# Both layers' overflow parts in front of their last groups, another passage between the layers and a shorter reciprocal root

## The chip, the cores and the metric

The kernel runs on one core of a Trainium2 chip. The metric is the device time of one execution in microseconds (us), the median of several. A profile is one further execution, recorded instruction by instruction. PE (TensorE) does matrix products and PEld its weight loads, DVE is VectorE, ACT is ScalarE, POOL is GpSimd, and SP is SyncE, which here only issues DMAs and reads addresses. [...]

## The reference

A backbone of two layers, 256 context tokens and 256 latent tokens of 1024 features, all in float32. Each layer is a token mixer and then a mixture of experts (MoE), both behind a modulated RMS norm and added to the stream through a gate row (`g2` is the MoE's, one row for the context tokens and one for the latent ones):

```python
def rmsnorm(t, g):
    y = t * rsqrt(mean(t * t, axis=-1) + 1e-6)
    return y * g

def hier_moe(h, ...):                 # 32 experts; each token gets 2 experts of its best group of 8
    for e in range(32):
        hid = silu(t @ w_gate[e]) * (t @ w_up[e])         # 1024 -> 256
        y = y + gates[:, e:e + 1] * (hid @ w_down[e])     # 256 -> 1024
    ...
# layer 0: context and latent tokens (512); layer 1: the MoE sees the latent tokens only (256)
x = x + g2 * hier_moe(modnorm(x, norm_g, sh2, sc2), ...)
# after both layers: rmsnorm(x, final_g)
```

## The kernel before

The stream `X` stays on the chip in tiles of 128 tokens: tiles 0 and 1 are the context, 2 and 3 the latent tokens. Layer 0's MoE works on four tiles (T = 4), layer 1's on two. An `Identity` matrix turns a 128x128 block on TensorE (`tr`, line 246); `mm` is an ordinary product (line 242).

**The MoE stage** is the loop over groups at the end of `tail` (from line 1528). A group is one product of 128 rows: two experts with 64 rows each (letters `s`, `p` of `SEQ`) or four with 32 rows each (`q`). Layer 0 has 13 groups, layer 1 has 11. Tokens are put into the rows by rank within their expert. `pair` (line 1731) does one group: the first products with the gate and up weights (PSUM tile `psg`), SiLU on ScalarE and a product on VectorE, `then` (the next group's rows, `rows(q + 1)`), the transposes of the hidden rows and their copy `hidT`, the down product (`psm`), the rows scaled by their gates and split into a high and a low part, and the products that bring the rows back to their tokens (`psc`), added to an accumulator `F` in each group but the last.

In the last group the local `gated()` (line 1542) multiplies the accumulated `F` by `g2` and adds it to `X`, a background step that `pair` issues behind the group's SiLU, and `add` (line 1549) takes the last group's own part: layer 1 has `g2` in the rows already (`cols`), layer 0 multiplies each returned 128x512 block by `g2` (line 1553) and adds it to `X` (line 1554), three of them on GpSimd (`SHARE`).

**The weights** come in units of 1 MB (three per expert: gate and up in two, down in one). `weights`, `pump` and `expert_load` (lines 1586 to 1592 and around) issue them on SyncE's DMA queue in the order of use, one as soon as a unit is given back by a product that is done with it. The first experts (`FIXED`) have a fixed place; the others are ordered by how many tokens they got, so SyncE reads each one's number from the chip's memory (`values_load`) before its first load.

**The overflow part** (`overflow`, line 1615) serves tokens whose rank lies above the rows of a group. It reads the largest count (line 1618), and under `tc.If(cnt > 64)` (line 1621) it goes through all 32 experts again, with the last five or six weight units as its memory, which it loads again at its end. In this run the count is below that and the body is skipped: each engine reads the count and jumps. What stands ahead of the `If` in the program is done ahead of it on each engine; the scheduler (Tile) that orders the instructions mixes nothing across it, and the semaphore counts that its body would move are brought up to date on the other path. Layer 0's is called at line 1497, ahead of group 0, where `F` is still empty (hence the branch `if not F`, which adds to `X` directly); layer 1's at line 1529, ahead of group 2 (`OVER`).

**Other work that the change touches.** `norm1` (line 439) makes the turned, normalised rows of all four tiles at the start of each layer: sum of squares, `rsqrt_`, scaling on VectorE (line 453), turning on TensorE, evacuation with the modulation. `rsqrt_` (line 169) is a reciprocal root on VectorE, an integer first guess and two steps of iteration, ten instructions on columns of one to ten numbers; `rms` feeds it, and `final` (line 1809) uses it for the output. `s5_prepare` is work for layer 1's mixer, laid into layer 0's last groups as background (`self.bg`); `prefetch1` starts layer 1's loads behind layer 0's last group.

Of the kernel before, what the change touches and what calls it, by code (L numbers as in the profile page):

```python
# [13 lines left out]
I32 = mybir.dt.int32  # L14
U32 = mybir.dt.uint32
AF = mybir.ActivationFunctionType
ALU = mybir.AluOpType
# [4 lines left out]
P = 128  # L22
# [6 lines left out]
OVER = (0, 2)  # L29
EARLY = (4, 4)  # L30
SHARE = ((0, 0), (1, 0), (2, 0))
# [130 lines left out]

def small(pool, name, n):

    return pool.tile([P, 10], F32, name=name, tag=name)[:, :n]


def rsqrt_(nc, pool, src, n, scale, src2=None):


    V = nc.vector
    x, y, t, q = (small(pool, "rs" + c, n) for c in "xytq")
    if src2 is None:
        V.tensor_scalar(x, src, float(scale), EPS, op0=ALU.mult, op1=ALU.add)
    else:
        V.scalar_tensor_tensor(x, src, EPS, src2, op0=ALU.add, op1=ALU.add)
    V.tensor_scalar(y.bitcast(I32), x.bitcast(I32), -0.5, float(0x5F375C00), op0=ALU.mult, op1=ALU.add)
    V.scalar_tensor_tensor(t, y, -0.5, y, op0=ALU.mult, op1=ALU.mult)
    V.tensor_mul(t, t, x)
    V.scalar_tensor_tensor(y, t, 1.5009, y, op0=ALU.add, op1=ALU.mult)  # L180
    V.tensor_mul(t, y, y)
    V.tensor_mul(t, t, x)
    V.tensor_scalar(q, t, 0.375, -1.25, op0=ALU.mult, op1=ALU.add)
    V.tensor_mul(q, q, t)
    V.scalar_tensor_tensor(y, q, 1.875, y, op0=ALU.add, op1=ALU.mult)
    return y
# [44 lines left out]
class Body:  # L231
# [193 lines left out]
    def rms(self, tiles, tmp):  # L425

        n = len(tiles)
        if n == 1:
            ss = small(self.sm, "ss", 2)
            for h in range(2):  # L430
                cs = slice(512 * h, 512 * h + 512)
                self.nc.scalar.activation(tmp[0], self.X[tiles[0]][:, cs], AF.Square, scale=1.0 / 32, accum_out=ss[:, h:h + 1])
            return rsqrt_(self.nc, self.sm, ss[:, 0:1], 1, 1.0, ss[:, 1:2])
        ss = small(self.sm, "ss", n)
        for j, i in enumerate(tiles):
            self.nc.scalar.activation(tmp[j], self.X[i][:], AF.Square, accum_out=ss[:, j:j + 1])
        return rsqrt_(self.nc, self.sm, ss, n, 1.0 / D)

    def norm1(self, layer):
# [9 lines left out]
        for b in range(2):  # L449
            xn = [next(ring) for _ in range(2)]  # L450
            r = self.rms([2 * b, 2 * b + 1], xn)
            for i in range(2):
                nc.vector.tensor_scalar(xn[i], self.X[2 * b + i][:], r[:, i:i + 1], None, op0=ALU.mult)  # L453
            for j in range(4):
# [3 lines left out]
                for k in range(4):  # L458
                    d, i = 2 * j + k // 2, k % 2
                    self.tr(ps[:, 128 * k:128 * k + 128], xn[i][:, 128 * d:128 * d + 128])  # L460
# [895 lines left out]
    def tail(self, layer, tiles, mix, mixT):  # L1356
# [5 lines left out]
        with ExitStack() as es:  # L1362
# [133 lines left out]
            if not local:  # L1496
                self.overflow(layer, h2d, T, None)
                ask(1)
# [28 lines left out]
            for q in range(nG):  # L1527
                if local and q == OVER[layer]:
                    self.overflow(layer, h2d, T, F)
# [7 lines left out]
                gate2 = lambda t: row(g2, 0 if local else t // 2)  # L1537
                if q == nG - 1:

                    def gated():  # L1540
                        for n, t in enumerate(tiles):
                            V.tensor_mul(F[n], F[n], gate2(t))
                            V.tensor_add(self.X[t][:], self.X[t][:], F[n])
                            yield
                    self.work(1000)
                    self.bg = gated()

                    def add(n, cs, ps):
                        t = tiles[n]
                        if local:  # L1550
                            V.tensor_add(self.X[t][:, cs], self.X[t][:, cs], ps)
                            return
                        V.tensor_mul(F[n][:, cs], gate2(t)[:, cs], ps)
                        (nc.gpsimd if (n, cs.start) in SHARE else V).tensor_add(self.X[t][:, cs], self.X[t][:, cs], F[n][:, cs])
# [5 lines left out]
                               (row(g2, 0), row(g2, 1)) if local and final else None, q == 0 and not local)  # L1560
# [54 lines left out]
    def overflow(self, layer, h2d, T, F):  # L1615
# [3 lines left out]
        last = 5 if F else 6  # L1619
        assert len(self.pre) - last >= self.first[OVER[layer]]  # L1620
        with tc.If(cnt > 64):  # L1621
# [4 lines left out]
            if layer == 0:  # L1626
                self.route_places(T)
            nc.gpsimd.memset(x, 0.0)
            if not F:
                g2 = self.pre[-6].f  # L1630
                for b in range(2):
                    self.mod_row(layer, b, 5, g2[:, D * b:D * b + D])

                def F(n, cs, ps):
                    V.tensor_mul(ps, g2[:, D * (n // 2):D * (n // 2) + D][:, cs], ps)
                    V.tensor_add(self.X[n][:, cs], self.X[n][:, cs], ps)
# [94 lines left out]
    def pair(self, q, xT, T, part, n, tokc, gate, F, work=0, after=0, then=None, cols=None, new=False):  # L1731
# [24 lines left out]
        self.cp(hidT, ps[:, :256].rearrange("p (k t) -> p k t", t=128))  # L1756
# [49 lines left out]
    def final(self):  # L1806
# [4 lines left out]
        for t in (2, 3):  # L1811
            u = self.unit()
            y.append(u.f[:, :D])
            for h in range(2):
                nc.scalar.activation(u.f[:, D:D + 512], self.X[t][:, 512 * h:512 * h + 512], AF.Square, scale=1.0 / 32, accum_out=ss[:, k:k + 1])
                k += 1
# [226 lines left out]
```

## Time and profile before

| | |
|---|---|
| median of 3 runs | 1200.01 us (1198.22 to 1200.25) |
| the profiled execution's own time | 1194.71 us |
| its span, first to last instruction | 1192.7 us |
| TensorE, VectorE, ScalarE, GpSimd busy | 91 %, 59 %, 27 %, 4 % of the span |
| granted TensorE clock, mean | 0.963 |
| DMA | 298.82 MB, mean 251 GB/s |
| layer 0's MoE groups | about 385 to 690 us |
| layer 1's MoE groups | about 943 to 1187 us |

The shares are means over stages with different limits; the page also cuts the span into 40 equal slices (29.8 us each), where a digit is the busy share in tenths. The chain of waits goes back from the last instruction, at each step to what released it. A timeline lists instructions of one engine in order of time: start, length, what it is (output <- inputs by the program's names, shapes), the count where several alike stand in a row, and the idle time ahead with what ended it. The view of one line gives for each queue and instruction the count, the ns (min/median/max), and the first and last start. A table of stretches gives start:end, length, the busy us of PE, PEld, DVE, ACT and POOL (with counts), the granted clock, the DMA share and GB/s. Groups give count | busy us, mean ns | idle us before, with the releaser.

### The profile page before, as it was taken

The page shows a single profiled execution, that of the slowest core. Times are in us where ns is not written, and L with a number is a line of the kernel's source. Part 1 is how long each engine was busy: PE and PEld are TensorE (multiplying, and loading weights), DVE is VectorE, ACT ScalarE, POOL GpSimd, SP SyncE. Part 2 cuts the span into 40 slices and gives each one's busy share as a digit, 9 for nine tenths or more (in the row PEclk, how much of TensorE's full clock was granted, in tenths as well). Part 3 has the DMA queues.
Part 4 walks back from the last instruction along what each step waited for, and adds up shares of the span by engine and source line. Part 5 has one row for each costly group of instructions (what it writes and reads, how often), then busy time and mean ns, then how long its engine had stood idle before and what let it go on. Part 6 is the DMA issues. An engine that isn't in the chain of part 4 may idle for free.

```text
span 1192.7 us, 17395 instructions
## 1 busy us (share of the span) xinstructions
PE 1087.7 (91%) x6528; PEld 560.3 (47%) x6528; DVE 699.0 (59%) x1915; ACT 319.2 (27%) x651; POOL 52.6 (4%) x64
## 2 busy tenths in 40 slices
PE   5999999999998899989989879999989899999975
PEld 2356556544456333334435246556665554444331
DVE  4876889558567375363453678857564554433324
ACT  3323212135123211120221065245442221212111
POOL 0001410000000100000000100010000000000000
PEclk9999999959999899999999889999989899999998
DMA  8777533640404589999798512345637285999994
GB/s 306 283 266 265 212 131 129 239 196 4 173 36 135 206 349 419 421 419 413 294 421 320 208 36 75 121 137 201 231 137 292 83 342 229 422 421 421 420 420 190
DMA packets 48601, 298.82 MB, mean 251 GB/s; under 512 B 6407, under 2 KB 8984, under 8 KB 15165
## 3 DMA queue, kind: packets, MB, share of 16 engines
q1 hardware_dynamic: 40380, 281.58, 60.4%
q10 hardware_dynamic: 5728, 11.86, 2.7%
q0 software_dynamic: 2400, 4.19, 1.0%
q8 instruction: 54, 0.88, 0.3%
q14 instruction: 39, 0.31, 0.1%
HBM read 295.68 MB, written 4.26 MB: 251 GB/s over the span
## 4 chain that ended last, share of the span: by engine, by line
PE 45%; DVE 10%; DMA 9%; ACT 2%; issue 1%; DVEq 0%; SPq 0%; ACTq 0%
PE psg L242 15%; PE psm L242 13%; PE psc L242 11%; DMA big<-w_e 9%; PE pst L242 3%; PE pst L246 2%; DVE big L1280 1%; PE psc L825 1%; DVE big L1216 1%; DVE big L1147 1%; DVE fr L1773 1%; ACT fr L1772 0%; DVE big L254 0%; ACT big L1155 0%; DVE big L1212 0%
## 5 line engine op out<-in xcount | busy, mean ns | idle before, releaser
L242 PE MATMUL psm<-big 128*128 128x512 f32 (+8 forms) x672 | 197.7, 466 | 4.6 <-ACT big L256 2.4
L242 PE MATMUL psg<-big,big 128*32 128x512 f32 (+1 forms) x720 | 176.6, 618 | 9.6 <-DMA big<-w_e 9.6
L242 PE MATMUL psm<-big,big 128*32 128x64 f32 (+7 forms) x600 | 129.2, 446 | 8.0 <-DVE big L254 4.1
L242 PEld LDWEIGHTS psm<-big 128*128 128x128 f32 (+2 forms) x672 | 91.3, 166 | 87.8 <-issue 64.7
L242 PE MATMUL psc<-big 128*32 128x32 f32 (+8 forms) x1108 | 111.6, 268 | 17.3 <-ACT big L514 7.8
L242 PE MATMUL psg<-big 128*64 128x512 f32 (+1 forms) x264 | 95.6, 617 | 8.1 <-PEq L1621 6.7
L242 PEld LDWEIGHTS psc<-big 128*32 128x32 f32 (+3 forms) x1108 | 73.7, 128 | 56.2 <-issue 29.7
L242 PE MATMUL psc<-fr 128*128 128x512 f32 x296 | 94.0, 431 | 4.1 <-DVE fr L1773 3.1
L1786 DVE TENSOR_TENSOR big<-big,psc 128x512 f32<-128x512 f32 x128 | 82.6, 684 | 22.0 <-PE psc L242 21.5
L246 PE MATMUL pst<-k_par,big 128*128 128x128 f32 (+2 forms) x470 | 80.5, 299 | 15.8 <-DVE big L453 3.7
L246 PEld LDWEIGHTS pst<-k_par,big 128*128 128x128 f32 (+2 forms) x470 | 55.8, 149 | 68.0 <-issue 30.1
L242 PEld LDWEIGHTS psc<-fr 128*128 128x128 f32 x296 | 49.5, 187 | 76.8 <-DVE big L1786 20.3
L242 PEld LDWEIGHTS psg<-big,big 128*32 128x32 f32 (+1 forms) x720 | 44.2, 124 | 86.2 <-issue 69.8
L242 PEld LDWEIGHTS psm<-big,big 128*32 128x32 f32 (+2 forms) x600 | 54.0, 145 | 51.8 <-issue 39.2
L1773 DVE SCALAR_TENSOR_TENSOR fr<-psm,tab,fr 128x512 fp32r<-128x512 f32 x46 | 34.6, 751 | 74.1 <-ACT fr L1772 71.7
L256 ACT ACTIVATE big<-pst 128x512 f32<-128x512 f32 (+2 forms) x88 | 47.3, 547 | 92.2 <-PE pst L246 85.0
L242 PE MATMUL psm<-parts 128*128 128x512 f32 x264 | 67.8, 405 | 0.5 <-DVE parts L651 0.5
L242 PE MATMUL psm<-big,bm 128*64 128x512 f32 (+1 forms) x256 | 56.4, 644 | 9.7 <-DVE bm L254 6.0
L242 PEld LDWEIGHTS psm<-parts 128*128 128x128 f32 x264 | 48.1, 188 | 19.0 <-issue 7.2
L1772 ACT ACTIVATE fr<-psm,tab 128x512 fp32r<-128x512 f32 x46 | 31.6, 687 | 70.9 <-PE psm L242 70.9
L242 PEld LDWEIGHTS psg<-big 128*64 128x64 f32 (+1 forms) x264 | 25.1, 131 | 48.5 <-issue 45.7
L1749 DVE TENSOR_TENSOR big<-big,psg 128x256 f32<-128x256 f32 x11 | 4.6, 420 | 72.3 <-ACT big L1748 72.3
(399 smaller groups left out, 1379.5 us busy)
## 6 DMA issues: line engine op xcount, KB each, us to landing
big<-w_e SPq DMA_DIRECT2D x187, 1024.0 KB, 15.8
big<-w_mod SPq DMA_DIRECT2D x36, 1024.0 KB, 5.1
x<-w_mod SPq DMA_DIRECT2D x12, 1024.0 KB, 4.9
big<-w_out SPq DMA_DIRECT2D x8, 1024.0 KB, 6.7
big<-w_hy SPq DMA_DIRECT2D x6, 1024.0 KB, 6.0
big<-modd ACTq DMA_DIRECT2D x10, 512.0 KB, 10.9
x<-w_e SPq DMA_DIRECT2D x5, 1024.0 KB, 13.6
h2d<-big ACTq DMA_DIRECT2D x6, 512.0 KB, 4.5
```

What stands on the lines that cost most here:

```text
L242: self.product = self.nc.tensor.matmul(out, lhsT, rhs, start=start, stop=stop)
L246: return self.nc.tensor.transpose(out, in_, self.ident[:k, :k])
L256: self.nc.scalar.activation(out, in_, AF.Copy)
L825: m = self.nc.tensor.matmul(ps[:, :k.shape[-1]], q, k, start=True, stop=True)
L1147: V.tensor_mul(sc[:, j, :].rearrange("p (d u v h) -> p d u v h", d=2, u=4, v=4), tab(x), bc_(c + y, perm))
L1216: V.scalar_tensor_tensor(v, self.iota[:, :128], self.s5l[:, ix(y):ix(y) + 1], v, op0=ALU.mult, op1=ALU.add)
L1280: V.tensor_tensor_scan(z, R[:, 16 * d + 4 * qq + q:16 * d + 4 * qq + q + 1].to_broadcast([P, 128]), z, 0.0, op0=ALU.mult, op1=ALU.add)
L1749: m = V.tensor_mul(hid, hid, ps[:, 256:])
L1772: nc.scalar.activation(hi, pd[hf][:], AF.Copy, scale=gate)
L1773: V.scalar_tensor_tensor(lo, pd[hf][:], gate, hi.bitcast(F32), op0=ALU.mult, op1=ALU.subtract)
L1786: V.tensor_add(F[t][:, cs], F[t][:, cs], ps[:])
```

## The change

- `OVER` goes from (0, 2) to (12, 10), and both layers call `overflow` from the loop: ahead of the last group, in layer 0 too, where `F` is then full. The branch for an empty `F` and layer 0's second call of `route_places` are gone.
- Layer 0's last group takes `g2` in its rows as layer 1's does: group 11 makes a row `gs` that has, for each of the last group's rows, the context's or the latent tokens' `g2` (by the token number), `pair` gets it as `cols`, and `add` is one addition on VectorE. `SHARE` is gone.
- In the last group of either layer the copy `hidT` goes to ScalarE (`"s"`).
- `norm1` scales the identity instead of the rows: a 128x128 diagonal matrix `dg` of the roots on VectorE, and a plain product of the tile with it, which turns and scales at once.
- `rsqrt_` carries the constants in the number itself (`HALF`, `MAGIC`): nine instructions, or seven for a single column, where `square()` takes one instruction for each column (up to two columns).

```diff
-OVER = (0, 2)
+OVER = (12, 10)
-SHARE = ((0, 0), (1, 0), (2, 0))
+HALF, MAGIC = 0.5 / 2.25, -554172480.0
 def rsqrt_(nc, pool, src, n, scale, src2=None):
+    def square():
+        for j in [slice(j, j + 1) for j in range(n)] if n <= 2 else ():
+            V.scalar_tensor_tensor(t[:, j], y[:, j], x[:, j], y[:, j], op0=ALU.mult, op1=ALU.mult)
+        if n > 2:
+            V.tensor_mul(t, y, y)
+            V.tensor_mul(t, t, x)
-        V.tensor_scalar(x, src, float(scale), EPS, op0=ALU.mult, op1=ALU.add)
+        V.tensor_scalar(x, src, float(scale * HALF), EPS * HALF, op0=ALU.mult, op1=ALU.add)
...
-    V.tensor_scalar(y.bitcast(I32), x.bitcast(I32), -0.5, float(0x5F375C00), op0=ALU.mult, op1=ALU.add)
-    V.scalar_tensor_tensor(t, y, -0.5, y, op0=ALU.mult, op1=ALU.mult)
-    V.tensor_mul(t, t, x)
-    V.scalar_tensor_tensor(y, t, 1.5009, y, op0=ALU.add, op1=ALU.mult)
-    V.tensor_mul(t, y, y)
-    V.tensor_mul(t, t, x)
-    V.tensor_scalar(q, t, 0.375, -1.25, op0=ALU.mult, op1=ALU.add)
-    V.tensor_mul(q, q, t)
-    V.scalar_tensor_tensor(y, q, 1.875, y, op0=ALU.add, op1=ALU.mult)
+    V.tensor_scalar(y.bitcast(I32), x.bitcast(I32), -0.5, MAGIC, op0=ALU.mult, op1=ALU.add)
+    square()
+    V.scalar_tensor_tensor(y, t, -1.5009, y, op0=ALU.add, op1=ALU.mult)
+    square()
+    V.scalar_tensor_tensor(q, t, -5.0 / 3, t, op0=ALU.add, op1=ALU.mult)
+    V.scalar_tensor_tensor(y, q, 1.25, y, op0=ALU.add, op1=ALU.mult)
 # norm1
+            dg = [x[:, :P] for x in xn]
-                nc.vector.tensor_scalar(xn[i], self.X[2 * b + i][:], r[:, i:i + 1], None, op0=ALU.mult)
+                nc.vector.tensor_scalar(dg[i], self.ident[:], r[:, i:i + 1], None, op0=ALU.mult)
-                    self.tr(ps[:, 128 * k:128 * k + 128], xn[i][:, 128 * d:128 * d + 128])
+                    self.mm(ps[:, 128 * k:128 * k + 128], self.X[2 * b + i][:, 128 * d:128 * d + 128], dg[i], True, True)
 # tail
             if not local:
-                self.overflow(layer, h2d, T, None)
                 ask(1)
...
-                if local and q == OVER[layer]:
+                if q == OVER[layer]:
                     self.overflow(layer, h2d, T, F)
...
+                if q == nG - 2 and not local:
+                    gs, m = row(xgu[0], nG % 2), small(self.sm, "branch", 2)
+                    for b, op in enumerate((ALU.is_le, ALU.is_gt)):
+                        V.tensor_scalar(m[:, b:b + 1], self.entry(nG - 1)[0], 256.0, None, op0=op)
+                    nc.scalar.activation(gs, row(g2, 0), AF.Copy, scale=m[:, 0:1])
+                    V.scalar_tensor_tensor(gs, row(g2, 1), m[:, 1:2], gs, op0=ALU.mult, op1=ALU.add)
...
-                        V.tensor_mul(F[n][:, cs], gate2(t)[:, cs], ps)
-                        (nc.gpsimd if (n, cs.start) in SHARE else V).tensor_add(self.X[t][:, cs], self.X[t][:, cs], F[n][:, cs])
+                        V.tensor_add(self.X[t][:, cs], self.X[t][:, cs], ps)
...
-                               (row(g2, 0), row(g2, 1)) if local and final else None, q == 0 and not local)
+                               None if not final else (row(g2, 0), row(g2, 1)) if local else (gs, row(xgu[0], (nG - 1) % 2)), q == 0 and not local)
 # overflow
-        last = 5 if F else 6
+        last = 5
-            if layer == 0:
-                self.route_places(T)
-            if not F:
-                g2 = self.pre[-6].f
-                for b in range(2):
-                    self.mod_row(layer, b, 5, g2[:, D * b:D * b + D])
...
 # pair
-        self.cp(hidT, ps[:, :256].rearrange("p (k t) -> p k t", t=128))
+        self.cp(hidT, ps[:, :256].rearrange("p (k t) -> p k t", t=128), "s" if after else None)
```

The sum of squares in `rms` and `final` takes `math.sqrt(HALF) / 32` as its scale where it was 1 / 32.

## Rows read from the trace of the kernel before

**Rows 1.** The page's 40 equal slices: what the DMA engines moved, GB/s

```profile
GB/s 306 283 266 265 212 131 129 239 196 4 173 36 135 206 349 419 421 419 413 294 421 320 208 36 75 121 137 201 231 137 292 83 342 229 422 421 421 420 420 190
```

**Rows 2.** Chain of waits that ended last, layer 1's last groups

```profile
1038.74 3.65 PE psm L242 x16
1077.23 3.65 PE psm L242 x16
1155.59 19.75 DMA big<-w_e
1175.38 3.63 PE psm L242 x20
```

**Rows 3.** Timeline of TensorE and VectorE, layer 0's last two groups

```profile
647.20 3.65 PE L242 MATMUL psm<-big,bm 128*64 128x512 f32 x14
667.46 2.35 DVE L1542 TENSOR_TENSOR big<-big 128x1024 f32<-128x1024 f32 x2
672.47 6.04 PE L242 MATMUL psm<-big,bm 128*64 128x512 f32 x16 [4.44 <-DVE bm L254]
```

**Rows 4.** Instructions of line 1621 (the skip), 382 to 394 us, and who waited

```profile
L1621 SPq EVENT_SEMAPHORE  x8: 17/17/17, 385.8 to 390.4; - x8
L1621 PEldq COMPARE_BRANCH  x1: 6357/6357/6357, 385.9 to 385.9; - x1
  PE psg L242: 6.7, 1
```

**Rows 5.** Table of stretches: busy us by engine, clock, DMA share, GB/s

```profile
392.60:397.50 4.90, 4.90 (x12) 1.57 (x14) 2.36 (x8) 0.00 (x0) 1.25 (x1) 0.51 0.18 47
690.00:703.80 13.80, 8.79 (x38) 6.05 (x39) 9.55 (x33) 5.99 (x13) 0.00 (x0) 0.75 0.23 78
```

**Rows 6.** Timeline of TensorE, layer 0's first group

```profile
392.56 6.05 PE L242 MATMUL psg<-big 128*64 128x512 f32 x16 [6.69 <-PEq L1621]
398.43 3.62 PE L242 MATMUL psg<-big,big 128*64 128x512 f32 x16
```

**Rows 7.** Line 1621 in layer 1, 982 to 999 us

```profile
L1621 SPq EVENT_SEMAPHORE  x9: 17/17/17, 987.9 to 997.8; - x9
L1621 PEldq COMPARE_BRANCH  x1: 409/409/409, 987.0 to 987.0; - x1
```

**Rows 8.** Line 1586 (reads of the expert order), 985 to 1007 us

```profile
L1586 SPq TENSOR_LOAD <-order x17: 262/263/274, 985.7 to 1005.2; - x17
```

**Rows 9.** Timeline of SyncE, 999 to 1010 us

```profile
1006.05 0.94 SPq L1592 DMA_DIRECT2D big<-w_e  x2
```

**Rows 10.** Stretches of 5 us behind layer 1's skip

```profile
995.00:1000.00 5.00, 4.63 (x38) 3.82 (x34) 2.02 (x6) 1.40 (x4) 0.00 (x0) 1.00 0.08 31
1000.00:1005.00 5.00, 4.76 (x19) 1.38 (x19) 2.94 (x11) 2.18 (x4) 0.00 (x0) 1.00 0.01 2
```

**Rows 11.** VectorE's groups by line and shape, 640 to 704 us

```profile
L1553 DVE TENSOR_TENSOR big<-big,psc 128x512 f32<-128x512 f32 x8 | 5.4, 684 | 1.5 <-PE psc L242 1.5
L1554 DVE TENSOR_TENSOR x<-x,big 128x512 f32<-128x512 f32 x5 | 3.4, 703 | 0.0
```

**Rows 12.** Timeline of VectorE, layer 1's last group

```profile
1178.18 1.61 DVE L1768 SCALAR_TENSOR_TENSOR big<-psm,tab,big 128x512 f32<-128x512 f32 x2 [3.97 <-PE psm L242]
```

**Rows 13.** Timeline of VectorE, passage to layer 1

```profile
689.26 0.69 DVE L1554 TENSOR_TENSOR x<-x,big 128x512 f32<-128x512 f32 x1
702.81 1.00 DVE L471 TENSOR_SCALAR big<-pst,A,B 128x256 f32<-128x256 f32 x2 [1.37 <-ACT big L469]
```

**Rows 14.** Timeline: 128x128 products on TensorE, a 128x128 scaling on VectorE

```profile
975.39 3.84 PE L242 MATMUL pst<-bm,x 128*128 128x128 f32 x32
365.78 0.28 DVE L1666 TENSOR_SCALAR bm<-k_par,big 128x128 f32<-128x128 f32 x1
```

**Rows 15.** Timeline of VectorE: a root's first step, and the scaling behind it

```profile
11.66 0.17 DVE L174 TENSOR_SCALAR rsx<-ss 128x2 f32<-128x2 f32 x1 [1.97 <-ACT big L436]
13.64 1.42 DVE L453 TENSOR_SCALAR big<-x,rsy 128x1024 f32<-128x1024 f32 x2
```

## What the change is predicted to do

> **What bounds the kernel now.** I read the page's slices first, then the chain of waits that ended last, then the lines of the overflow passage, then the order of time around them. The two mixture-of-experts stages (about 385 to 690 us and 943 to 1187 us) load all experts' weights, and the slices show 413 to 422 GB/s in most of them [rows 1]: the loads run at one rate, 1 MB in some 2.5 us. Which engine ends last differs. In layer 1 the chain's last 78 us (from 1097 us) are weight loads laid end to end, and the last product starts at 1175.38 us when the last load lands [rows 2]. Two groups earlier the TensorE beat is (1077.23 - 1038.74) / 2 = 19.2 us a group [rows 2]. Counted from 1077.23, the last group's product (four groups on) would start at about 1154 to 1156 us with its weights there, so TensorE has some 20 us to spare at the end, and whatever makes the load stream earlier by less than that is worth its full length. In layer 0 it is TensorE that is busy end to end from 392 us on, until the last group, where it stands still 4.4 us behind VectorE [rows 3].
>
> The overflow part is skipped in this run, but the skip costs in four places. [...] In layer 1 the jump takes 0.41 us only, but SyncE, which issues the weight loads, waits on nine counters from 987.9 to 997.8 us until every load in flight has landed [rows 7]; then it makes the rest of the 17 reads of the expert order [rows 8], and only at 1006.05 does the next load go out [rows 9]. The DMA engines stand at 31 and 2 GB/s meanwhile [rows 10].
>
> **The change part by part.**
>
> *Layer 0's skip leaves its place in front of group 0.* Gone are the 6.7 us of idling, less 0.3 us in which the next product would start anyway, and the clock's loss of 6.05 - 3.62 = 2.4 us [rows 4, 6]: -8.8 us. The group's rows and weights lie ready there; the loads that follow are released by TensorE's own progress, so they move with it. Bounds: -6 (clock falls all the same) to -9.2.
>
> *It comes back in front of group 12.* Between the second-last group's down product, which ends at 647.20 + 3.65 = 650.85, and the end of the last one's at 672.47 + 6.04 = 678.51, there are 27.7 us now [rows 3]. In them the last group's first products run among the second-last group's adds; the passage is one block, so nothing is mixed across it. Afterwards, one after the other: the adds of group 11 (eight of 0.68 us and the start of the chain, 7.0), reading the count (0.5), the jump (6.4 as at the old place), the start (0.3), the rest of the S5 preparation (3.0, what lies among the adds now), 32 first products (7.2, twice the 16 of [rows 6]), the clock's fall (2.4), gate, transpose and copy (2.3), the down product at full clock (3.65): 32.7 us, so +5.0. (The small terms are from the timeline of the same stretch.) In that sum the change has already taken out two things: the copy of the hidden rows goes to ScalarE, so it no longer queues behind VectorE's 4.7 us of gating [rows 3], and the product behind it runs at full clock, not 6.04 us. The gating itself fits in the jump and the first products. VectorE's own jump, and SyncE's wait for landing loads, lie beside TensorE's. What SyncE holds back there are layer 1's first loads, due 25 us later; the last expert loads are issued before. [...]
>
> [...]
>
> *The gates in the rows (layer 0's last group).* Eight multiplies (5.4 us) and five adds on VectorE (3.4 us, three more on GpSimd) [rows 11] become eight adds; the half products pass through one more VectorE step of about 0.8 us each, as layer 1's last group has it (1.61 us for two) [rows 12]. From the down product's end to the last add: 689.95 - 678.51 = 11.4 us now [rows 3, 13]; afterwards two gated products 1.6, two remainders 1.4, eight adds of 0.68 = 5.5, and 0.8 of hand-over: 9.3, so -2.1. The new gate row costs 1.1 us on ScalarE and 1.2 us on VectorE in group 11, beside its products. Bounds: 0 to -3.5.
>
> *The passage to layer 1.* From the last add (689.95) to the last evacuation (703.81) it is 13.9 us [rows 13], at three quarters of the clock [rows 5]. Afterwards: square and its sum 1.4, the root in nine steps of 0.2 = 1.8, two small scalings of 0.28 [rows 14], then four PSUM tiles at 0.9 us and one evacuation 0.6: 8.4 us, so -5.5. The first pair's tiles are through before. A plain product costs TensorE what the transpose did: 32 of 128x128 take 3.84 us [rows 14]. Bounds: -2.5 (if it stays at half clock and the evacuation sets the pace) to -7.5.
>
> *The shorter root.* Ten steps take 1.98 us (11.66 to 13.64) [rows 15]; one column saves three (0.6 us), two to ten columns one (0.2). On the path lie layer 1's last routed tile (0.6), and about half of the eight others (0.4): -1.0. At the start, four scalings of 0.71 us [rows 15] become four of 0.28, and VectorE's chain sets the pace until 46 us: -1.5 (0 to -2.1).
>
> *Layer 1's skip leaves its place in front of group 2.* SyncE would no longer wait ten microseconds; the 17 order reads of 0.58 us with their arithmetic run from 985.7 to about 995.5 [rows 8], and then the load goes out that now waits until 1006.05 [rows 9]: -10.5 us for the stream. The buffers are there: six loads leave back to back from 1006.05 on, and the first four of their buffers are free by 995.6 (group 2's first products end then); the later ones come free at least 2 us before the stream needs them. So the 12 us hole [rows 10] closes to about 2. Bounds: -2 (only TensorE's own 2 us, if buffers held it) to -12.
>
> *It comes back in front of group 10.* TensorE's jump (0.4 us) and the lost overlap (some 4 us) lie beside the wait for the weights: 20 us to spare less 10.5. SyncE's wait delays nothing but the output's stores, 10 us later. On ScalarE's queue the output norm's row, loaded at 1136 us now, goes out behind the skip and is needed at 1183; GpSimd's gathers are all in layer 0 and issued before its skip. Value 0; the bound is the first rival.
>
> **The sum**: -8.8 + 5.0 - 2.1 - 5.5 - 1.0 - 1.5 - 10.5 = -24.4 us. The profiled execution took 1194.7 (span 1192.7 and 2.0 around it), so 1170.3 by its own time. The median of the runs shown is 1200.0, 5.3 above it; the same offset gives 1175.6, and I say 1176.
>
> **The rivals.**
> (1) *The last loads may be used only when all have landed.* The body that is skipped would reload the last five loads, so who reads those buffers behind the skip waits until SyncE has brought the counters up to date, in a fixed order, each after its last load landed. If the order of the counters isn't the order of landing, most of layer 1's last first product (3.5 us, and 1.2 of clock), gate and copy (2.4) and the down product (3.65) come after the last landing, 10.8 us in place of 3.6 [rows 2]: +7 to 8, 1184. For it: the nine waits in a row [rows 7]. Against: it needs an unlucky order. 25%.
> (2) *The hole stays*: buffers or the order reads hold the stream, and only 2 of the 10.5 us are won: 1184.5. Against: six loads back to back [rows 9]. 9%.
> [...] 8%.
> (4) *Slower: the jump's code waits behind weight loads.* In layer 1 a load takes 19.8 us from issue to landing [rows 2]. If the code is fetched behind such a queue at both new places, layer 0 pays 20 in place of 6.4 (+13.6) and layer 1's last group starts 20 us late, 11 of them beyond the slack, with 2.4 of clock: +27, 1203. It decides once the wait is over 18 us in both. Against: layer 0's last loads are landed by then, and the old jump took 6.4 us with two loads in flight. 4%.
> [...]
>
> **How the numbers follow.** The forecast has 54%, its own range 1170 to 1182 from the bounds above; rivals (1) to (3) at 1184 or so have 42%, (4) has 4%. The range for eight in ten reaches from 1168 (both gains of layer 1 and the passage at their far bounds) to 1188 (the first rival with a second microsecond of code fetch behind). What a measurement can tell is about 0.2%, 2.4 us: faster 0.94, the same 0.02, slower 0.04.
>
> **What would show it.** In the changed profile: no idle time of TensorE at 386 and no half clock behind it; DMA over 400 GB/s through layer 1's groups 2 and 3, without a slice near zero; layer 0's idle time of 5 to 7 us now ahead of its last group; no wait of the hidden rows' product for VectorE there; 8 to 9 us from the last add to layer 1's first projection; and at the end one chain of loads, with 3.6 us of down product behind the last landing. I am wrong if TensorE's last first products in layer 1 lie behind the last load, if the hole in the stream is there at another place, or if layer 0's last group loses more than 9 us.

## The result, and the profile after

The changed kernel took **1180.39 us** in the median of its first runs (1179.13 to 1197.42), the kernel before 1198.22 beside it: a ratio of 0.987 (95% interval 0.984 to 0.990). Run once more on another chip it took 1186.23 against 1196.3, a ratio of 0.992 (0.990 to 0.995). The 1197.42 is a run in a slower state of the chip (granted TensorE clock 0.948 of full speed, 0.955 to 0.968 in the other four), which the ratio leaves out. So the kernel is faster by 9 to 16 us by the two ratios, the range on record holds it, and the 24 us of the sum are not there.

The profiled execution took 1188.44 us, its span is 1186.7: only 6.0 below the first trace of before. The first 390 us blur the comparison, since the same instructions took more or less time there in each run (last section). So I count from one row that all kernels have, the last small products of the routing right ahead of layer 0's experts. Timeline of TensorE, first the changed kernel, then a second trace of the kernel before:

```profile
390.71 1.10 PE L249 MATMUL psc<-R,big 128*64 128x4 f32 x32
```
```profile
386.93 1.10 PE L242 MATMUL psc<-R,big 128*64 128x4 f32 x32
```

From there to the end it is 1186.7 - 390.7 = **796.0 us** in the changed kernel (795.9 in its second trace). Before it is 807.9 in the first trace (the row starts at 384.76) and 808.8 in the second (1195.7 - 386.9). The change is worth **12 to 13 us** behind this row. The two kernels that were traced twice agree with themselves to 1 us over the whole of it; single stages differ by up to 2.3 us between two traces of one kernel.

Now the stages. The page's slices, as [rows 1]:

```profile
GB/s 312 281 249 254 243 50 165 206 278 1 177 36 68 272 366 425 426 426 392 290 424 288 244 38 74 124 112 209 234 136 311 72 334 373 400 427 425 427 424 79
```

Layer 1's stream stands in slices 33 and 34 and after: the 342 and 229 of before are 334 and 373 now. Layer 0's head, timeline of TensorE, as [rows 6]: no idle time, and both halves of the first products at full clock (1.00 granted from 391.7 to 398.7 us).

```profile
391.67 3.63 PE L249 MATMUL psg<-big 128*64 128x512 f32 x16
395.13 3.60 PE L249 MATMUL psg<-big,big 128*64 128x512 f32 x16
```

The skip (line 1631 now) ahead of layer 0's last group, 640 to 670 us, as [rows 4]; then who waited:

```profile
L1631 PEldq COMPARE_BRANCH  x1: 3951/3951/3951, 656.5 to 656.5; - x1
L1631 DVEq COMPARE_BRANCH  x1: 72/72/72, 657.2 to 657.2; - x1
L1631 DVEq EVENT_SEMAPHORE  x1: 21/21/21, 663.0 to 663.0; - x1
  PE psg L249: 6.8, 1
```

TensorE's jump takes 4.0 us, but VectorE's next instruction comes 5.8 us behind its own, and TensorE's first product waits for that. The stretches, as [rows 5 and 10]: the idle time, the fallen clock behind it (0.56 granted), the weight stream where the hole was, the last group.

```profile
656.40:663.40 7.00, 0.18 (x2) 0.11 (x2) 1.27 (x3) 0.00 (x0) 0.00 (x0) 0.74 0.81 301
663.40:667.00 3.60, 3.60 (x10) 2.04 (x12) 3.60 (x4) 0.00 (x0) 0.00 (x0) 0.56 0.03 11
995.00:1000.00 5.00, 4.38 (x29) 2.43 (x29) 3.33 (x13) 1.83 (x4) 0.00 (x0) 1.00 1.00 423
1000.00:1005.00 5.00, 5.00 (x19) 1.71 (x16) 3.48 (x5) 1.37 (x2) 0.00 (x0) 1.00 1.02 431
1150.50:1162.00 11.50, 0.01 (x1) 0.00 (x0) 0.00 (x0) 0.00 (x0) 0.00 (x0) 0.53 0.83 350
```

The last row is the surprise: all engines stand still for 11.5 us in front of the end. Timeline of TensorE there, and SyncE's counters in line 1631 (1143 to 1165 us):

```profile
1149.46 1.05 PE L249 MATMUL psg<-big,big 128*32 128x512 f32 x2 [1.39 <-DMA big<-w_e]
1162.05 5.02 PE L249 MATMUL psg<-big,big 128*32 128x512 f32 x26 [11.55 <-SPq L1631]
1168.91 3.64 PE L249 MATMUL psm<-big,big 128*32 128x512 f32 x32 [0.47 <-ACT big L263]
```
```profile
L1631 SPq EVENT_SEMAPHORE  x8: 17/17/17, 1161.6 to 1162.1; - x8
```

The last load goes out at 1141.7 (1155.6 before, [rows 2]). SyncE's eight counters move in one stroke at 1161.6, when it has landed. (A ninth count, SyncE's own, moves at 1142.3, right behind its jump.) Only then does TensorE go on, and more slowly at first: 5.0 us for 26 products, which take 3.6 in e1 below (granted clock 0.53 while it stood, 0.76 from 1162 to 1168).

### The profile page after: what moved, and what is told of

The parts are those of the page before. It is cut to its first block, busy times and chain, and to the rows that moved or that the text cites. A ratio compares the mean times of both kernels' runs of the same rounds, so it can differ in the third digit from the quotient of the medians.

```text
span 1186.7 us, 17505 instructions
## 1 busy us (share of the span) xinstructions
PE 1082.6 (91%) x6592; PEld 570.0 (48%) x6592; DVE 690.9 (58%) x1880; ACT 320.8 (27%) x654; POOL 48.3 (4%) x61
## 5 line engine op out<-in xcount | busy, mean ns | idle before, releaser
L249 PE MATMUL psg<-big,big 128*32 128x512 f32 (+1 forms) x720 | 172.2, 612 | 15.4 <-SPq L1631 11.5
L249 PE MATMUL psm<-big,big 128*32 128x64 f32 (+7 forms) x600 | 125.1, 438 | 7.1 <-DVE big L261 3.1
L249 PE MATMUL psc<-big 128*32 128x32 f32 (+8 forms) x1108 | 112.3, 268 | 20.4 <-ACT big L522 10.5
L253 PE MATMUL pst<-k_par,big 128*128 128x128 f32 (+1 forms) x406 | 67.9, 291 | 6.7 <-DVE big L826 1.7
L253 PEld LDWEIGHTS pst<-k_par,big 128*128 128x128 f32 (+1 forms) x406 | 46.1, 143 | 50.9 <-issue 29.0
L249 PEld LDWEIGHTS pst<-bm,x 128*128 128x128 f32 x352 | 43.4, 204 | 7.5 <-issue 6.6
## 6 DMA issues: line engine op xcount, KB each, us to landing
big<-w_e SPq DMA_DIRECT2D x187, 1024.0 KB, 12.8
```

The source lines that it names most:

```text
L249: self.product = self.nc.tensor.matmul(out, lhsT, rhs, start=start, stop=stop)
L253: return self.nc.tensor.transpose(out, in_, self.ident[:k, :k])
```

## The experiments

Eleven kernels. "To the end" is the time from the row named above; it is the finer measure, as the medians move with the first 390 us (those of the changed kernel differ by 6). But it comes from one trace of each kernel, so differences of about 1 us say nothing. By the ratios alone only e10 and e11 stand clear of the changed kernel; the other intervals overlap with its two.

| kernel | median us | ratio to before (95%) | to the end us |
|---|---|---|---|
| before (two traces, the second e12) | 1195.7 to 1198.2 | 1 | 807.9, 808.8 |
| changed (two traces, the second e9) | 1180.4, 1186.2 | 0.987, 0.992 | 796.0, 795.9 |
| e1 other order of counters | 1177.3 | 0.985 (0.980 to 0.989) | 789.7 |
| e2 layer 1 without overflow | 1177.4 | 0.983 (0.979 to 0.987) | 788.2 |
| e3 layer 0 without overflow | 1174.1 | 0.981 (0.977 to 0.986) | 790.8 |
| e4 layer 1's at its old place | 1185.6 | 0.989 (0.985 to 0.994) | 798.8 |
| e5 layer 0's at its old place | 1187.0 | 0.993 (0.990 to 0.995) | 796.8 |
| e6 old scaling in norm1 | 1183.8 | 0.991 (0.988 to 0.994) | 797.7 |
| e8 shorter body in layer 0 | 1181.4 | 0.990 (0.987 to 0.993) | 795.0 |
| e10 looped body, other order | 1174.2 | 0.981 (0.979 to 0.984) | 785.7 |
| e11 the same, earlier root | 1172.9 | 0.981 (0.979 to 0.984) | 785.3 |

**Why the end waits.** My theory was the first rival of the prediction, with the order of the counters as its cause. Loads take eight counters in turn; SyncE brings them up to date in a fixed order behind the skip, and the last load of layer 1 happens to sit on the first (so it stands in the built program). One load less in the rotation puts it on the last:

```diff
-        nc.scalar.dma_start(g.f[:, :D], I["ngrow"][4:5, :].to_broadcast([P, D]))
+        nc.gpsimd.dma_start(g.f[:, :D], I["ngrow"][4:5, :].to_broadcast([P, D]))
```

> The changed kernel, with one small load (the output norm's row) on GpSimd's queue instead of ScalarE's. It is one load less on the rotating counters, so the last weight load of layer 1 counts on the counter that SyncE brings up to date last behind the skip (in the changed kernel: on the first). Theory: the last group's products wait only because SyncE's first counter in order is that of the last load. Then the 11.6 us of TensorE's idle time ahead of the last first products go, the end is some 17.5 us behind the last landing in place of 25.1, and the time is 7 to 8 us below the changed kernel's 1180.4, about 1173. Rival: the products behind the skip need all loads landed in whatever order: no change, 1180. Second rival: the skip's code and its place in the order of work hold them: 1178 to 1180, with the idle time shorter but the end as far behind the last landing.

Timeline of TensorE in e1, the last group, and its SyncE row (1135 to 1160 us):

```profile
1141.49 1.04 PE L249 MATMUL psg<-big,big 128*32 128x512 f32 x2 [1.38 <-SPq L1631]
1144.05 3.59 PE L249 MATMUL psg<-big,big 128*32 128x512 f32 x26 [1.52 <-SPq L1631]
1153.68 3.62 PE L249 MATMUL psm<-big,big 128*32 128x512 f32 x26 [1.39 <-SPq L1631]
```
```profile
L1631 SPq EVENT_SEMAPHORE  x8: 17/17/17, 1136.7 to 1153.6; - x8
```

The counters now move as the loads land, over 17 us and not in one stroke. The idle time is cut into waits of at most 1.5 us, and only the down product's last 3.6 us lie behind the last landing (1153.6, so 17.8 us to the end; 25.1 in the changed kernel). To the end it is 6.3 us less, a little under the 7 to 8 expected; the median, 1177.3, stays 4 above the 1173 expected. The rivals fall: neither must all loads be landed, nor is it the skip itself.

```diff
-                if q == OVER[layer]:
+                if q == OVER[layer] and not local:
```

> The changed kernel without layer 1's overflow part (it computes no overflow of layer 1). Theory (order of the counters): the same as the kernel with the other order of counters, within 1.5 us, about 1172 to 1173: TensorE's own jump (0.4 us) and the work that it keeps apart lie beside the wait for weights. Rival: the skip costs by itself too (2.0 us of TensorE's idle time ahead of it, no overlap): 2 to 4 us lower than that, 1169 to 1171.

Timeline of TensorE in e2, the end of the down product:

```profile
1164.10 3.62 PE L249 MATMUL psm<-big,big 128*32 128x512 f32 x20 [0.53 <-DMA big<-w_e]
```

Here it waits for the load itself, and the end comes 17.1 us behind (1181.2 - 1164.1). Without layer 1's overflow the time to the end is 7.7 us below the changed kernel, 1.5 below e1. With the right order the skip is hidden but for that, which is little more than two traces of one kernel differ by. The median, 1177.4, is again 4 to 5 above what was expected.

**What the two places cost.** e4 has `OVER = (12, 2)`; e5 has layer 0's call and its branch for an empty `F` back as in the kernel before; e3 skips layer 0's call (`and local`).

> The changed kernel with layer 1's overflow part back in front of group 2 (layer 0's stays in front of group 12). Theory: the hole in the weight stream is back (the last load lands 11 to 12 us later than in the changed kernel), and the last group's wait for the counters is gone (7.7 us): +3 to +4.5, about 1184. Rival: the stream was earlier for another reason than the hole; then only the wait goes, 1173.

Stretches of e4, and the end of its chain of waits:

```profile
990.00:995.00 5.00, 5.00 (x22) 1.79 (x20) 0.00 (x0) 0.00 (x0) 0.00 (x0) 0.84 0.00 2
995.00:1000.00 5.00, 5.00 (x38) 3.69 (x35) 1.17 (x3) 0.84 (x2) 0.00 (x0) 1.00 0.00 0
```
```profile
1147.18 19.27 DMA big<-w_e
1166.49 3.63 PE psm L249 x20
```

The hole is back. The last load lands at 1166.5 - 384.9 = 781.6 us behind the mark, against 1161.6 - 390.7 = 770.9 in the changed kernel: the hole costs 10.7. Behind the landing it is 17.1 us to the end, not 25.1. Together +2.8, just under what was expected; the rival (-7) falls.

> The changed kernel without layer 0's overflow part (it computes no overflow of layer 0). It prices the skip in front of group 12. Theory: TensorE's 6.8 us of idle time, and the 3 us that the first products take longer at the fallen clock go, less about 2 us for VectorE's gating that lies beside the jump now: 6 to 8 us below the changed kernel, 1172 to 1174. Rival: VectorE's adds and gating hold the last group anyway, as they did before the change: -2, 1178.

The down products of groups 11 and 12 on TensorE, first in the changed kernel, then in e3:

```profile
645.35 3.65 PE L249 MATMUL psm<-big,bm 128*64 128x512 f32 x14
674.00 3.65 PE L249 MATMUL psm<-big,bm 128*64 128x512 f32 x16 [0.53 <-ACT bm L263]
```
```profile
639.63 2.31 PE L249 MATMUL psm<-big,bm 128*64 128x512 f32 x8
659.67 3.66 PE L249 MATMUL psm<-big,bm 128*64 128x512 f32 x16 [0.53 <-ACT bm L263]
```

From the end of the one to the end of the other it is 28.65 us with the skip and 21.4 without, so the skip costs 7.3 us there. In the trace of e3 the first products of the last group run among the adds of the one before, without idle time. To the end it gains 5.2 us (it has lost 1.4 in the groups ahead).

> The changed kernel with layer 0's overflow part back in front of group 0 (layer 1's stays in front of group 10). By the stages of the traces: the head of layer 0 gives back 9.2 us, the last group gets the 7.3 us that the skip costs there (changed kernel against the one without it): +1.9 us against the changed kernel run beside it. By the prediction's own terms it would be +3.8 (8.8 less 5.0). Rival: the skip ahead of the last group hides behind nothing and before group 0 its cost was hidden partly: -2 or lower.

At the old place TensorE's jump took 7.2 us. Head and last group together come to +2.5 (9.73 more in the head, 7.26 less in the last group) where +1.9 was expected; to the end it is +0.9, and the median is 0.8 above e9's beside it. Layer 0's move is worth 2.5 us by its stages, not 3.8, and the time to the end doesn't tell it from nothing.

**Why the passage to layer 1 didn't get shorter.** e6 has the rows scaled and turned as in the kernel before.

> The changed kernel with the rows scaled on VectorE and turned by the identity in norm1, as before the change. The prediction gave the other passage 5.5 us between the layers and part of 1.5 us at the start: then this is 6 to 7 us slower than the changed kernel beside it. Theory after the first traces: the passage takes 13.9 us from the last add to the last evacuation in both, so it is TensorE at its half clock and the evacuations one after the other that set its length: within 1.5 us of the changed kernel, and the trace shows 13 to 15 us for this passage.

From the last add to the last evacuation: 13.7 us in e6, 13.9 and 13.4 in the two traces of before, 12.8 to 13.9 with the diagonals in nine traces. To the end e6 is 1.8 us slower, but not by the passage: at its last evacuation e6 stands 309.1 us behind the mark, between the changed kernel's two traces (310.2 and 308.8). Its median is 2.4 us below that of the changed kernel beside it (1183.8 and 1186.2, with intervals that overlap). So the new scaling is worth 0 to 1 us in the passage, and nothing that these runs show in the whole. Timeline of TensorE and then VectorE in the changed kernel, as [rows 13]:

```profile
689.15 7.93 PE L249 MATMUL pst<-big,x 128*128 128x128 f32 x48 [2.12 <-DVE big L461]
```
```profile
686.96 0.16 DVE L184 TENSOR_SCALAR rsx<-ss 128x2 f32<-128x2 f32 x1
688.72 0.48 DVE L461 TENSOR_SCALAR big<-k_par,rsy 128x128 f32<-128x128 f32 x2
700.37 0.54 DVE L479 TENSOR_SCALAR big<-pst,A,B 128x256 f32<-128x256 f32 x1 [0.35 <-ACT big L477]
```

The scalings are short as foreseen (0.48 us for two, 1.42 before). But the first pair's root starts only as the last add ends (686.96; 687.04), so all eight PSUM tiles come behind it, 64 products and sixteen evacuations, and these set the length. The 48 products that take 7.9 us here (0.165 us each) run in part at a lower clock (0.69 granted from 689 to 693 us, 0.88 from 687 to 701). In e9 the clock stayed full there (1.00; 16 products in 2.05 us, 0.13 each), and the passage still took 12.8 us, as the products then wait for evacuations, 0.34 us ahead of the 16 (timeline of TensorE in e9, 686 to 702 us):

```profile
692.65 2.05 PE L249 MATMUL pst<-big,x 128*128 128x128 f32 x16 [0.34 <-DVE big L479]
```

**Why layer 0's skip costs what it does.**

```diff
-                for r in range(T):
+                for r in range(T if layer else 1):
```

> The changed kernel with a shorter overflow body in layer 0: one of the four groups of rows of each expert stands in the loop (the overflow of the other three is left out). Nothing that is executed changes, only the length of the code that is jumped over. Theory: the jump's cost is the fetch of code that lies far away; with about a third of the body VectorE's 5.7 us and TensorE's 4.0 us at the skip fall to 1 us or less, as in layer 1, TensorE idles under 2.5 us there, its clock doesn't fall, and the time is 5 to 7 us below the changed kernel. Rival: the stall is the wait for counters and queues at a skip in layer 0, whatever its length: no change.

Line 1631 in e8, first layer 0 (646 to 650 us), then layer 1, and TensorE's timeline in layer 0's last first products:

```profile
L1631 PEldq COMPARE_BRANCH  x1: 353/353/353, 647.8 to 647.8; - x1
L1631 DVEq EVENT_SEMAPHORE  x1: 21/21/21, 649.1 to 649.1; - x1
L1631 PEldq COMPARE_BRANCH  x1: 5796/5796/5796, 1127.9 to 1127.9; - x1
```
```profile
652.83 1.12 PE L249 MATMUL psg<-big 128*64 128x512 f32 x1 [2.16 <-issue]
```

TensorE's jump and VectorE's restart are short in layer 0 (0.35 and 0.6 us), TensorE stands 1.6 us for it and then 2.2 us more for nothing that the trace shows, and its products slow down all the same: 1.12 us for one that takes 0.59 later, as behind the changed kernel's idle time (1.08 at 0.56 granted). Between the ends of the two down products it is 26.8 us, against 28.65 and 29.4 in the changed kernel's two traces: 1.8 to 2.6 us won there, not 5 to 7. And layer 1's jump, over a body that is unaltered and at the same place, takes 5.8 us where it took 0.41 in the changed kernel; in e4 it takes 6.35, at the old place, where it took 0.41 in the kernel before. So one body was jumped in 0.41, 5.8 and 6.35 us, and its length alone doesn't give the time; between the changed kernel and e8 only code ahead of it differs. What takes the time in a long jump, a fetch of code or something else, is not shown here.

> The changed kernel again, unaltered, so that the others stand beside it on the same chip: 1180 by its first runs. Its first 290 us should end anywhere within 11 us, as in the traces so far (381.8 to 393.0 us at the start of layer 0's experts), and from there on each stage should take what it took in the first trace within 1.5 us: skip ahead of group 12 with 6.8 us of TensorE's idle time, last landing to end 25 us.

It came out so (11.6 us of idle time ahead of the last first products, 25 us from landing to end).

**A version that beats both.** e10 takes e1's order, and runs the body's groups of rows as a loop; e11 also issues the first root behind the adds of tile 1.

```diff
-                for r in range(T):
-                    self.gather(x, h2d, T, self.slot_index(tq[:, r, 0:1], 1)[0][:])
+                with tc.For_i(0, T) as r:
+                    V.tensor_copy(t1, tq[:, ds(r, 1), :].rearrange("p r a -> p (r a)"))
+                    self.gather(x, h2d, T, self.slot_index(t1[:, 0:1], 1)[0][:])
...
+                        if not local and (n, cs.start) == (1, 512):      # e11, in add()
+                            self.r0 = self.rms([0, 1], [F[0], F[1]])
```

> The changed kernel with the other order of the counters (the output norm's row on GpSimd's queue), and with the groups of rows of an expert in the overflow body as a loop that the chip runs in place of four (two in layer 1) copies in the code. Nothing that is executed changes, and nothing is left out. Theory: both gains of the single runs add: TensorE idles 1.6 to 2.5 us at the skip ahead of group 12 in place of 6.8 and its clock stays up (-3 to -5), and the wait ahead of the last group's products is gone (-7.4): 10 to 12.5 us below the changed kernel, that is a ratio to the kernel before of 0.977 to 0.980 where the changed kernel had 0.987 and 0.992. Rival: layer 1's jump becomes long where the code has moved (6.8 us as with the shorter body) and is no longer hidden: 3 us of it are given back at the end.

> As the kernel with the looped body and the other order of counters, and besides the first root of layer 1's norm1 (context tiles 0 and 1) is issued on VectorE right behind those two tiles' last adds, ahead of the latent tiles' adds. Theory: the passage didn't get shorter because the first pair's root stands behind the last add in VectorE's order, so all eight PSUM tiles come after it. Then the first product of the passage starts at 0.6 to 1 us behind the last add in place of 2.1, and the last evacuation comes 1.2 to 3 us earlier (12.8 to 13.9 us in the changed kernel, so 10.5 to 12.3): 1 to 3 us below the kernel with the looped body. Rival: the passage is bound by TensorE at half clock for 64 products and 8 evacuations, whenever it starts; the root that now stands between the adds delays them by 1.7 us and nothing is won.

Line 1631 in e10, layer 0, and its last group's down product in layer 1:

```profile
L1631 PEldq COMPARE_BRANCH  x1: 3712/3712/3712, 654.1 to 654.1; - x1
L1631 DVEq EVENT_SEMAPHORE  x1: 21/21/21, 655.4 to 655.4; - x1
```
```profile
1156.67 3.62 PE L249 MATMUL psm<-big,big 128*32 128x512 f32 x26 [1.40 <-SPq L1631]
```

VectorE's restart fell from 5.8 to 0.6 us, TensorE's jump stayed at 3.7 and its products behind it slowed down (1.06 to 1.09 us each, 0.59 where 1.00 is granted): 27.2 us between the two down products, so 1.4 to 2.2 won there, less than the 3 to 5 expected. With the order of counters it is 10.3 us to the end, the lower edge of what was expected, and the ratio, 0.981, just misses its 0.977 to 0.980; the rival's long jump in layer 1 did not come (0.33 us). e11's first product starts 1.6 us behind the last add, not 0.6 to 1, the last evacuation 12.3: the root, which takes its sums of squares from ScalarE, starts at 676.28 us, when the latent tiles' adds are nearly done (the last one starts at 677.01). It gains 0.4 us to the end, which can't be told from nothing. Both kernels are below the changed one and some 22 us below the one before.

> The kernel before once more, for a second trace of it. Theory: its first 290 us move from run to run by TensorE's clock as those of the changed kernel do (381.8 to 393.0 us at the start of layer 0's experts, 384.8 in the first trace of before), and from there on every stage takes what it took in the first trace within 1.5 us.

Start at 386.9 us, and from there each stage within 1.5 us but for layer 0's first twelve groups, which took 2.3 more; the last group took 1.0 less (26.65 us between the two down products).

## Why the prediction was right or wrong

The time fell into the range, but by its ratio to the kernel before (0.987 and 0.992) it stands with the first rival (1184 of 1200.0 is 0.987) and not with the forecast (1176, 0.980). That 1180.4 also lies in the forecast's own 1170 to 1182 is luck: half of the sum did not come, and the mechanism failed at the end and in the passage. Step by step, from the offsets between the first two traces:

- **Layer 0's head**: -8.8 predicted, -9.2 measured (offset +5.95 at the mark, -3.29 behind the first products). Right.
- **The skip ahead of group 12**: +5.0 predicted, between the ends of the two down products; 677.65 - 649.0 = 28.65 against 27.7, so +1.0 (+2.8 in the second traces, 29.4 against 26.65). The steps were right, four sizes too large: the adds with the S5 preparation among them took 8.5 us (10.5 counted, one after the other), the restart 5.8 (6.7), the first products with the fallen clock (0.56 granted from 663.4 to 667) 8.8 (9.6), gate and copy 1.9 (2.3). The down product took its 3.65. The skip alone costs 7.3 (e3).
- **The gates in the rows**: -2.1 predicted; 687.04 - 677.65 = 9.4 against 11.4: -2.05. Right.
- **The passage to layer 1**: -5.5 predicted, 0 to -1 measured, outside its bounds. The step that failed is "The first pair's tiles are through before". They weren't before the change either; what went was VectorE's scaling, and what is late next is TensorE's products and the evacuations of eight tiles. (The terms given for it also add up to 8.0 us and not to 8.4.)
- **The shorter root, and the start**: -1.0 and -1.5 predicted. The root's steps shrank, but neither shows. Up to layer 1's second down product 1.4 us are lost (978.44 in place of 979.92, where the offset was -2.9 at 700; 1.6 in the second traces); the skip that is gone ahead of group 2 gives 1.4 back. Part of the loss is TensorE's clock ahead of layer 1's first group, whose 28 products that fetch rows take 6.28 us now and took 5.38 before (granted clock 0.50 from 935.6 to 946.4 us, and 0.55 from 938 to 948 before; the rows stand below the list). At the start 1.8 us are won by 17 us (16.70 in place of 18.48 for the same product) and lost again before 60 us; the start of layer 0's experts lies between 381.8 and 393.0 us in ten traces with the new root and scaling, at 384.8 and 386.9 in two without. Why these stretches grew stays open.
- **The hole in layer 1's stream**: -10.5 predicted. The last load lands at 1161.6 in place of 1175.4 while the offset was -2.9 at 700: -10.9 (-9.4 in the second traces); e4 says 10.7. Right.
- **The skip ahead of group 10**: 0 predicted, +7.7 measured (25.1 us from the last landing to the end against 17.4). This is the failed step that counts. "SyncE's wait delays nothing but the output's stores" is wrong: behind the skip the readers of the last five units wait for SyncE's counters, 11.55 us in one piece. The first rival had both the mechanism and the price (+7 to 8), and I gave it 25% because I took the unlucky order for chance. It is fixed in the program and could have been read there. Rival 2 fell with the hole, rival 3 (no net gain in layer 0) in that layer 0 did gain (-9.2, +1.0 and -2.05 by its parts), rival 4 with jumps of 4.0 and 0.41 us; even the long jumps of layer 1, 5.8 us in e8 and 6.35 in e4 (426 and 336 GB/s in the two stretches from 980 to 990 us), are far from the 18 us that it needed. No run shows what a fetch of code costs, which the range's upper end (1188) takes in; the runs show these jumps in its place.

Timeline of TensorE, the 28 products ahead of layer 1's first group, in the changed kernel (930 to 948 us) and in the kernel before:

```profile
940.39 6.28 PE L249 MATMUL pst<-bm,x 128*128 128x128 f32 x28 [0.72 <-DVE bm L1691]
```
```profile
942.76 5.38 PE L242 MATMUL pst<-bm,x 128*128 128x128 f32 x28 [0.72 <-DVE bm L1691]
```

Taken together, +7.7 at the end, some +5 in the passage, 2.5 for root and start and 1.4 lost in layer 0's groups (traces of one kernel differ there by as much), against 4 us less for group 12's skip and 0.8 more at head and hole, turn -24.4 into about -12.6, and the traces show -12 to -13 behind the mark. These sizes are of one pair of traces; the two that count, the end and the hole, are far above what traces of one kernel differ by.

## What to carry to other kernels

The skipped conditional was not free here (TensorE's jump took from 0.33 us in e10's layer 1 to 7.2 in e5's layer 0): ask of each engine how long it jumps and when its next instruction comes, and of the DMA queue which counters it must bring up to date, in which order, and who reads the buffers that the skipped body would write. Moving it to where one engine has slack moved the wait onto the last group, and which transfer sits on which counter decided 6.3 us (e1; 7.7 in e2, without the skip). When a scaling is taken off the path, count all the tiles that come behind the last input, not those of the last half.

## What the runs showed of the hardware

- The jump over the same body of layer 1 took TensorE 0.41 us in the kernel before, in the changed one and in e1, and 5.8 us in e8, where against the changed kernel only code ahead of it differs; in e4, at the old place, it took 6.35. Over e10's looped body it took 0.33.
- The first 290 us vary by 11 us between runs with the same instructions there (layer 0's experts start between 381.8 and 393.0 us), and the granted clock differs in them. The same stretch, at 0.77 and at 0.89 granted, in the changed kernel and in e1:

```profile
240.00:300.00 60.00, 54.61 (x213) 25.29 (x210) 39.46 (x142) 25.20 (x74) 0.00 (x0) 0.77 0.31 122
```
```profile
240.00:300.00 60.00, 54.58 (x234) 25.67 (x234) 42.72 (x146) 29.70 (x85) 0.00 (x0) 0.89 0.31 124
```

The idle time of 2.9 us at 159 us in the changed kernel came with a fallen clock (0.64 of full speed granted in 160 to 165); the same idle time in the first trace of the kernel before did not (2.9 us, 1.00). From 120 to 180 us 0.94 was granted in the changed kernel, and 1.00 in e1, with the same instructions. Stages have to be compared from a common row behind such places, not by spans.
